# Moving the attention loop of a hybrid encoder layer into the hand-placed plan, with the S5 linear unit woven into its first two steps

## The chip, the cores and the metric

The kernel runs on one NeuronCore of one Trainium2 chip. The metric is the device time of one execution in microseconds (us); the time before is 1659.16 us, the median of three runs (1657.36 to 1663.84).

## What is computed

One post-norm layer over 1024 tokens of width 1024, all in fp32:

```python
h = layer_norm(x)
rq, rk, rv, rg, su, aq, ak, av = split(h @ w_in)
y_ret = retention(rq, rk, rv, rg, theta)              # 256 columns
y_ssm = s5_mixer(su, ...)                             # 256 columns
#   y = gelu(C states + D u);  y * sigmoid(y @ w_glu + b_glu)
y_att = window_sink_attention(aq, ak, av, sink)       # 512 columns
#   8 query heads on 2 key heads; a block of 128 queries sees its own and both
#   neighbouring key blocks; m = max(scores, sink);  p = exp(scores - m)
#   y = (p / (sum(p) + exp(sink - m))) @ v
h = layer_norm(alpha * h + concat(y_ret, y_ssm, y_att) @ w_out)
aff = softmax(h @ router_w)                           # 16 experts
# every expert takes its 128 tokens of highest affinity: SwiGLU, times gate, added back
h = layer_norm(alpha * h + experts(h))
```

## The kernel before

A matrix product that needs fp32 precision is made of three: each operand is split into a high and a low part (`split`, L60: ACT copies the high part, L65, and DVE subtracts it for the low part, L66), and `mm3` (L72) issues high·high, high·low and low·high (L74 to L76). TensorE also makes the transposes, into one PSUM tile `tp` of 128x512 (two buffers). PSUM has two buffers `at` for scores, two `mm` for projections, one `po` for attention values and one `sm` for the router.

The program has three parts. **The front**, `front()`, is a `Plan`: each operation is entered with `at(place, operation)`, and the sorted places are the program order of all engines, issued under a manual schedule. It ends with the units V0, o0, K0, o1, V1, o2, K1, o3: projections of keys and values, and four quarters of the S5 output (class `Output`). A quarter `o` multiplies transition tiles `MU` and `W` (L807, L810) with the saved states `Z`, which `Output.states` loads from DRAM (`s_d`) on SP's queue (L799). At places from `G` on come the S5 linear unit: `turn` (L822 transposes, L823 copies), `gate` (L828, two products), `gated` (tanh on ACT, L836; L837 and L838 on DVE give `YO`), `store` (L842, to `y_d`), and the splits of the output matrix `WO` (class `Matrix`, `parts`). The first scores of attention blocks 0 and 1 also stand there, and their exponentials behind the linear unit.

**The loop** in `build` (L2202 on) has no hand-made order: it lists 17 iterations, and the timeline scheduler orders each engine's instructions. A block i (0 to 15) is one chunk of 128 queries and one key head, four query heads. `attention_scores` makes the scores (L1310, L1311); DVE adds the slope bias and takes the maximum (L1314, called TTR below), then the negated maximum and the sink term (L1317, L1318). `attention_exp` is ACT's exponentials with their sums (L1328, L1330). `attention_out` has DVE add and invert the sums (L1340, L1341), ACT scale the probabilities (L1343), PE transpose them per key block (L1349) with a split into `pT`, PE multiply with the values (L1356), and ACT and DVE put the result in the rows `yh`, `yl` (L65, L66, L1362). `out_proj_load(t)` loads the retention and S5 columns of tile t and splits them into the same `yh`, `yl`; `out_proj_part(t, n)` makes one half of 512 columns, 8 chunks of three products, and DVE adds the residual into `z` (L1391) with its statistics (L1394); `router(t)` transposes `z` (L1444, L1446 into `rt`), multiplies with the router's weights (L1456), computes the affinities (L1464 to L1473), finishes the norm (L1478 gain, L1483 shift) and stores, with ACT's scaled copy `ah` (L1492) in the buffer of `rt`; `rank_tile(t)` counts for expert choice (L1584 to L1595). I write half (t, n) for an out-projection half; there are 14 in the loop, (0,0) to (6,1).

**The rest** is `last_tile` (tile 7) and the experts, again by hand: `for` each of 16 experts, load, split, multiply.

Of the kernel before, what the change touches and what calls it, by code (L numbers as in the profile page):

```python
# [764 lines left out]
class Output:  # L765


    def __init__(self, K, I):
# [61 lines left out]

    def gated(self, m, q):
# [107 lines left out]
def front(K, I, pool, close):  # L939
# [314 lines left out]
    at(G + 1.2, lambda: mat.parts(4))  # L1254
    at(G + 5.0, lambda: mat.parts(6))
# [40 lines left out]
def attention_scores(K, i):  # L1296

    nc = K.nc
    c, kv = divmod(i, 2)
    b0, b1 = max(c - 1, 0), min(c + 2, NT)  # L1300
    W, ro, k0 = (b1 - b0) * P, (b0 - c + 1) * P, b0 * P
    qs = K.Q.pop(i)
    sm = K.small.tile([P, 5, 4], F32, name="asm", bufs=3)
    m, nm, rs, es, rd = (sm[:, k] for k in range(5))
    hs = slice(kv * 4, kv * 4 + 4)
    S = []
    for g in range(4):
        h = kv * 4 + g
        ps = K.pat.tile([P, 512], F32, name="at")
        nc.tensor.matmul(ps[:, :W], qs[:, g, :], K.KHL[kv][:, 0, k0:k0 + W], start=True, stop=False)  # L1310
        nc.tensor.matmul(ps[:, :W], qs[:, g, :], K.KHL[kv][:, 1, k0:k0 + W], start=False, stop=True)  # L1311
        s = K.score[K.heads % 10]
        K.heads += 1
        nc.vector.tensor_tensor_reduce(s[:, :W], ps[:, :W], K.R[:, ro:ro + W], 2.0 ** -(h + 1),  # L1314
                                       K.sink[:, h:h + 1], OP.add, OP.max, accum_out=m[:, g:g + 1])
        S.append(s)
    nc.vector.tensor_scalar(nm, m, -1.0, None, op0=OP.mult)  # L1317
    nc.vector.tensor_tensor(es, K.sink[:, hs], m, OP.subtract)  # L1318
    K.P[i] = S, sm
# [12 lines left out]

def attention_out(K, i):
    nc = K.nc
    c, kv = divmod(i, 2)
# [8 lines left out]
    po = K.po.tile([P, 512], F32, name="po")
    pTs = []
    for b in range(b0, b1):
        pt = K.ptp.tile([P, 4, P], F32, name="tp")
# [4 lines left out]
        pTs.append(pT)
    for b in range(b0, b1):
        pT = pTs[b - b0]
        for s in range(2):
# [8 lines left out]

def out_proj_load(K, t):
    nc, pool = K.nc, K.op
    y = pool.tile([P, 4, P], F32, name="y")
    nc.sync.dma_start(y[:, 0:2, :], K.y_dram[t])
    for m in range(2):
        nc.sync.dma_start(y[:, 2 + m, :], K.y2_dram[m][:, t * P:(t + 1) * P])  # L1370
    z = pool.tile([P, D], F32, name="z", bufs=3)
    rows = nc.sync.dma_start(z, K.h_dram[t])
# [4 lines left out]
    return rows


def out_proj_part(K, t, n, c0=0, c1=KC):  # L1380

    nc = K.nc
    yh, yl, z = K.Y[t]
# [3 lines left out]
    for c in range(c0, c1):
        mm3(nc, K.ps, (yh[:, c], yl[:, c]), [K.WO[s][c // 4][:, c % 4, ns] for s in range(2)], c == 0, c == KC - 1)
    if c1 < KC:
        return  # L1390
# [945 lines left out]
```

## Time and profile before

| | |
|---|---|
| runs | 1659.16 us median; 1657.36, 1659.16, 1663.84 |
| profiled execution | 1658.7 us |
| its span (first to last instruction) | 1657.0 us |
| mean granted TensorE clock | 0.988 of 2.4 GHz |
| front, up to the last product of o3 | 0 to 280.7 us |
| from there to the first out-projection half | 280.7 to 324.2 us |
| halves (0,1) to (6,1) | 326.8 to 472.5 us |
| last tile and experts | 472.5 to 1657 us |

Read it with the clock in mind: the change touches 250 to 475 us of the 1657, and the busy shares of the whole span are those of the experts. "Busy" of TensorE (PE) is the union of its rows, each with the tail of a pipelined matmul.

### The profile page before, as it was taken

The numbers are of one execution on the slowest core, as the hardware profiler recorded it, in microseconds if no ns is written. First come the engines' busy times: TensorE is split into PE (matmuls) and PEld (weight loads), VectorE is DVE, ScalarE is ACT, GpSimd is POOL, SyncE is SP. The second block draws the span as 40 slices with busy tenths as digits, with TensorE's granted clock in tenths as the row PEclk, the third lists the DMA queues.
The fourth block names the chain that finished last, engine by engine and source line by source line (L and its number), as shares of the span: only waits on it lengthen the run. The fifth ranks groups of instructions, "written<-read, shape, count | busy, mean of one in ns | idle before, by whom it ended". The sixth has DMA issues, their size and how long they took to land.

```text
span 1657.0 us, 21108 instructions
## 1 busy us (share of the span) xinstructions
PE 1587.8 (96%) x7704; PEld 1288.8 (78%) x7704; DVE 1416.3 (85%) x1734; ACT 1129.3 (68%) x1272; POOL 211.4 (13%) x237
## 2 busy tenths in 40 slices
PE   7999998799988999999999999999999999999997
PEld 5888886687766788888888888888888778777785
DVE  7986954777889989888898888888888999999996
ACT  4644544775646678777777777777778777787773
POOL 3002110011010010110101001010011303231221
PEclk9999999899999999999999999999999999999998
DMA  5566485324228899999999999999999999999993
GB/s 190 186 168 143 114 234 179 128 78 159 69 103 314 341 376 407 394 365 381 365 391 385 356 386 367 396 372 360 396 370 404 399 392 409 388 414 380 389 418 141
DMA packets 102682, 505.74 MB, mean 305 GB/s; under 512 B 12977, under 2 KB 28081, under 8 KB 51890
## 3 DMA queue, kind: packets, MB, share of 16 engines
q1 hardware_dynamic: 87426, 476.60, 75.3%
q0 software_dynamic: 15152, 27.79, 6.2%
q8 instruction: 60, 0.98, 0.2%
q14 instruction: 44, 0.36, 0.1%
HBM read 461.36 MB, written 42.99 MB: 304 GB/s over the span
## 4 chain that ended last, share of the span: by engine, by line
PE 60%; DVE 15%; DMA 9%; issue 7%; ACT 7%; POOL 1%; SPq 0%; POOLq 0%; DVEq 0%; ACTq 0%
PE gu L1812 27%; PE y L1812 14%; DVE whl L1859 6%; DMA zz<-acc_d 4%; PE mm L74 4%; PE mm L76 4%; PE mm L75 4%; ACT whl L1852 3%; DMA wraw<-in_exp_w_down 2%; PE tp L1797 2%; DMA wraw<-in_exp_w_gate 1%; PE po L1356 1%; ACT S L1330 1%; DVE pT L66 1%; PE sm L1456 1%
## 5 line engine op out<-in xcount | busy, mean ns | idle before, releaser
L1859 DVE TENSOR_TENSOR whl<-wraw,whl 128x2048 fp32r<-128x2048 f32 x384 | 873.4, 2289 | 94.1 <-ACT whl L1852 93.8
L1852 ACT ACTIVATE whl<-wraw 128x2048 fp32r<-128x2048 f32 x384 | 734.8, 1917 | 240.1 <-PE gu L1812 86.6
L1812 PE MATMUL gu<-whl,xT 128*128 128x512 f32 x3072 | 740.1, 397 | 0.0
L1812 PEld LDWEIGHTS gu<-whl,xT 128*128 128x128 f32 x3072 | 570.8, 189 | 124.7
L1812 PE MATMUL y<-whl,hT 128*128 128x512 f32 x1536 | 368.6, 395 | 0.7 <-ACT hT L65 0.7
L1812 PEld LDWEIGHTS y<-whl,hT 128*128 128x128 f32 x1536 | 288.5, 188 | 69.6 <-ACT hT L65 0.9
L1786 POOL DMA_INDIRECT xs<-h_d,index x15 | 41.4, 2758 | 740.5 <-PE y L1812 552.2
L65 ACT ACTIVATE hT<-tp 128x512 fp32r<-128x512 f32 x80 | 46.1, 584 | 31.7 <-PE tp L1797 17.0
L74 PE MATMUL mm<-hT,whl 128*128 128x512 f32 x160 | 65.9, 412 | 0.0
L76 PE MATMUL mm<-hT,whl 128*128 128x512 f32 x160 | 62.9, 393 | 0.0
L75 PE MATMUL mm<-hT,whl 128*128 128x512 f32 x160 | 62.6, 391 | 0.0
L66 DVE TENSOR_TENSOR hT<-tp,hT 128x512 fp32r<-128x512 f32 x80 | 54.1, 684 | 7.3 <-ACT hT L65 7.3
L74 PE MATMUL mm<-WO,yh 128*128 128x512 f32 x128 | 52.1, 407 | 3.5 <-ACT yh L65 3.5
L1797 PE MATMUL tp<-ident,hid 128*128 128x128 f32 x256 | 39.7, 279 | 13.5 <-DVE hid L1894 13.4
L1797 PEld LDWEIGHTS tp<-ident,hid 128*128 128x128 f32 x256 | 31.6, 142 | 25.1 <-DVE hid L1894 17.8
L75 PE MATMUL mm<-WO,yh 128*128 128x512 f32 x128 | 50.9, 398 | 0.0
L76 PE MATMUL mm<-WO,yl 128*128 128x512 f32 x128 | 49.6, 398 | 0.0
L74 PE MATMUL mm<-whl,hT 128*128 128x512 f32 (+1 forms) x128 | 46.4, 362 | 0.0
L1330 ACT ACTIVATE S<-S,asm 128x384 f32<-128x384 f32 (+1 forms) x64 | 36.9, 578 | 13.1 <-DVE asm L1317 7.6
L1894 DVE TENSOR_TENSOR hid<-hid,gu 128x512 f32<-128x512 f32 x64 | 43.6, 681 | 1.9 <-PE gu L1812 1.9
L76 PE MATMUL mm<-whl,hT 128*128 128x512 f32 (+1 forms) x128 | 43.5, 340 | 1.2 <-DVE hT L66 1.2
L75 PE MATMUL mm<-whl,hT 128*128 128x512 f32 (+1 forms) x128 | 43.7, 341 | 0.8 <-DVE whl L130 0.8
(430 smaller groups left out, 1775.4 us busy)
## 6 DMA issues: line engine op xcount, KB each, us to landing
wraw<-in_exp_w_gate SPq DMA_DIRECT2D x128, 1024.0 KB, 8.0
wraw<-in_exp_w_up SPq DMA_DIRECT2D x128, 1024.0 KB, 7.8
wraw<-in_exp_w_down SPq DMA_DIRECT2D x128, 1024.0 KB, 8.0
wraw<-in_w_in SPq DMA_DIRECT2D x8, 1024.0 KB, 7.2
x<-in_x SPq DMA_DIRECT2D x8, 512.0 KB, 4.6
h_d<-x SPq DMA_DIRECT2D x8, 512.0 KB, 3.2
q_d<-kst SPq DMA_DIRECT2D x32, 128.0 KB, 2.7
wraw<-in_w_out SPq DMA_DIRECT2D x4, 1024.0 KB, 5.8
```

Source lines behind the costliest of these rows:

```text
L65: nc.scalar.activation(hi, src, AF.Copy)
L66: eng.tensor_tensor(lo, src, hi.bitcast(F32), OP.subtract)
L74: nc.tensor.matmul(ps, a[0], b[0], start=start, stop=False)
L75: nc.tensor.matmul(ps, a[0], b[1], start=False, stop=False)
L76: nc.tensor.matmul(ps, a[1], b[0], start=False, stop=stop)
L1330: nc.scalar.activation(S[g][:, :W], S[g][:, :W], AF.Exp, bias=nm[:, g:g + 1], accum_out=rs[:, g:g + 1])
L1786: nc.gpsimd.indirect_dma_start(out=xs, out_offset=None, in_=K.h1_dram, in_offset=bass.IndirectOffsetOnAxis(ap=K.index[:, e:e + 1], axis=0))
L1797: K.nc.tensor.transpose(pt[:, c, :], src[:, (c0 + c) * P:(c0 + c + 1) * P], K.ident)
L1812: nc.tensor.matmul(ps, a[s][c], u[:, t, i * w:(i + 1) * w], start=first and id(ps) not in began, stop=last and left[id(ps)] == 0)
L1852: self.K.nc.scalar.activation(u[:, 0, :], self.raw[k1].rearrange("p a b -> p (a b)"), AF.Copy)
L1859: self.K.nc.vector.tensor_tensor(u[:, 1, :], raw, u[:, 0, :].bitcast(F32), OP.subtract)
L1894: at(self.after, q, 3, lambda: nc.vector.tensor_tensor(self.h[q], self.h[q], self.pg[q][1], OP.mult))
```

## The change

The loop moves into the plan. Z is the place behind o3. A new class `Block` splits a block's work into `scores` (two heads at a time), `top`, `exp`, `norm`, `scale`, `turn`, `part`, `value` and `put`, each entered with a place of its own; step j (2 to 15) begins at place Z + 20 + 11(j - 2). In step j stand the scores of block j+2, norm and scale of block j+1, turn to put of block j, one out-projection half in three pieces (t = j//2 - 1, n = j mod 2), one half of the router work of the tile before it, and in even steps the rank of the tile before that. Blocks 0 and 1 and the linear unit share the places Z to Z + 20. The last tile's function takes over the rank of tile 5.

```diff
@@ Output, states and their loads
-    def states(self, g2, q, pool):
+    def states(self, g2, q, pool, **kw):
...
-        z = pool.tile([P, 2, 4, P], F32, name="Z")
+        z = pool.tile([P, 2, 4, P], F32, name="Z", **kw)
@@ front
     at(e2 + 7.0, lambda: out.states(*qs[0], X["s5m"][1]))
+    at(e2 + 7.1, lambda: out.states(*qs[1], K.ast, tag="k4", bufs=3))
...
-    at(O + 0.02, lambda: out.states(*qs[1], X["s5o"][1]))
...
-    for i, k in enumerate(mq):
-        at(G + 1.7 + i * 2.0, lambda k=k: out.gate(*k))
-        at(G + 3.7 + i * 2.0, lambda k=k: out.gated(*k))
-    at(G + 11.0, lambda: (out.store(0), out.store(1)))
-    at(G + 15.0, lambda: close(X["s5o"][0], X["s5m"][0]))
+    for k, a, b in zip(mq, (3.6, 5.3, 9.6, 13.7), (5.4, 7.1, 11.4, 15.5)):
+        at(Z + a, lambda k=k: out.gate(*k))
+        at(Z + b, lambda k=k: out.gated(*k))
+    at(Z + 15.6, lambda: (out.store(0), out.store(1)))
...
-    at(G + 1.2, lambda: mat.parts(4))
-    at(G + 5.0, lambda: mat.parts(6))
+    at(Z + 4.5, lambda: mat.parts(4))
+    at(Z + 10.0, lambda: mat.parts(6))
...
-        at(G - 0.2 + i * 1.1, lambda i=i: attention_scores(K, i))
-        at(G + 10.4 + i * 2.6, lambda i=i: attention_exp(K, i))
+    scored(0, Z - 0.2, Z - 0.1, Z + 1.6, Z + 2.5)
+    scored(1, Z + 2.6, Z + 2.7, Z + 4.0, Z + 7.3)
+    at(Z + 6.0, block[0].norm)
+    at(Z + 6.2, lambda: block[0].scale(nc.vector))
+    turned_over(0, (Z + 8.7, Z + 8.8), Z + 12.7, Z + 16.2)
+    scored(2, Z + 11.3, Z + 11.4, Z + 13.0, Z + 13.5)
...
+    at(Z + 16.0, loop_space)
...
+    for j in range(2, 2 * NT):
+        s = Z + 20.0 + 11.0 * (j - 2)
+        k, odd = divmod(j, 2)
+        if j + 2 < 2 * NT:
+            scored(j + 2, s, s + 4.2, s + 5.2, s + 5.6)
...
+            at(s + 0.05, block[j + 1].norm)
+            at(s + 2.4, block[j + 1].scale)
+        turned_over(j, (s + 0.7, s + 1.15, s + 4.1), s + 8.35, s + 9.7)
+        t = k - 1
+        cs = (4, 5, 6, 7, 0, 1, 2, 3) if j == 2 else range(KC)
+        for place, a, b in ((1.6, 0, 3), (5.3, 3, 6), (6.95, 6, 8)):
+            at(s + place, lambda t=t, odd=odd, cs=cs, a=a, b=b: out_proj_chunks(K, t, odd, cs[a:b], a == 0, b == KC))
+        at(s + 8.4, lambda t=t, odd=odd: out_proj_end(K, t, odd))
...
+        else:
+            at(s + 6.6, lambda t=k: out_proj_split(K, t))
...
+            at(s + 3.7, lambda t=t: router_turn(K, t, 0))
+            at(s + 6.9, lambda t=t: router_part(K, t, 0))
+            at(s + 9.75, lambda t=t: router_turn(K, t, 1))
...
+            at(s + 1.55, lambda t=t: router_part(K, t, 1))
+            at(s + 2.3, lambda t=t: logits(K, t))
+            at(s + 3.2, lambda t=t: out_proj_gain(K, t))
+            at(s + 4.3, lambda t=t: logits_exp(K, t))
+            at(s + 6.5, lambda t=t: logits_norm(K, t))
+            at(s + 6.6, lambda t=t: out_proj_shift(K, t))
+            at(s + 8.0, lambda t=t: out_proj_store(K, t))
...
+            at(s + 7.0, lambda t=t: (token_parts(K, t), rank_tile(K, t)))
@@ build
-    for i in range(2 * NT + 1):
-        if ahead <= i < 2 * NT:
...
-            attention_scores(K, i)
-            attention_exp(K, i)
```

`scored(i, a, b, c, d)` places a block's two pairs of scores, `top` and `exp`; `turned_over` its turns (each with its split 0.5 later), values and `put`. Other edits: the probabilities of blocks 0 and 1 are scaled by DVE (L1436 of the new file) in place of ACT; `g1`, `b1` and the first expert weights are loaded from places in steps 3 and 9; the split of `y` is apart from its load.

**SP's queue, the loads of Z.** Before, behind the last store of `roT`; the pair for o1 is the first two Z rows, and the pair for o0 stands some ten rows higher:

```order
L431 DMA y_d_72<-roT 128x256
L775 DMA wg<-in_ssm_w_glu 128x512
L777 DMA bg<-in_ssm_b_glu 128x2
L788 DMA MU<-m_d_94 128x512
L789 DMA MU<-u_d 128x512
L792 DMA W<-wo_d_86 128x576
L792 DMA W<-wo_d_88 128x576
L799 DMA Z<-s_d_89 128x512
L799 DMA Z<-s_d_91 128x512
L799 DMA Z<-s_d_90 128x512
L799 DMA Z<-s_d_92 128x512
```

Now the pair for o1 stands right behind that for o0:

```order
L890 DMA q_d_1_76<-kst 64x512 x4
L799 DMA Z<-s_d_89 128x512
L799 DMA Z<-s_d_91 128x512
L799 DMA Z<-s_d_89 128x512
L799 DMA Z<-s_d_91 128x512
L431 DMA y_d_70<-roT 128x256
L431 DMA y_d_71<-roT 128x256
L890 DMA q_d_1_78<-kst 64x512 x4
L903 DMA wraw<-in_w_out 128x2048
L431 DMA y_d_72<-roT 128x256
```

It has moved past the stores of `roT`, the store of keys (`kst`), a load of the output matrix and the loads of `wg` to `W`.

**ACT, the first two steps** (L836 is the linear unit's tanh, `WO` the split of the output matrix, L1330 and now L1425 the exponentials, L1343 the scale). Before:

```order
L65 ACTIVATE WO_3093<-wraw 128x1024 x2
L836 ACTIVATE glu<-mm,hb 128x512
L65 ACTIVATE WO_3093<-wraw 128x1024 x2
L836 ACTIVATE glu<-mm,hb 128x512 x3
L1328 ACT_TABLE_LOAD
L1328 ACTIVATE asm<-asm 128x4
L1330 ACTIVATE S,asm<-S,asm 128x256 x4
L1328 ACTIVATE asm<-asm 128x4
L1330 ACTIVATE S,asm<-S,asm 128x256 x4
L1343 ACTIVATE S<-S,asm 128x256 x8
```

Now, from the linear unit's second pair on:

```order
L836 ACTIVATE glu<-mm,hb 128x512 x2
L1423 ACTIVATE asm<-asm 128x4
L1425 ACTIVATE S,asm<-S,asm 128x256 x4
L65 ACTIVATE pT<-tp 128x512 x2
L65 ACTIVATE WO_3105<-wraw 128x1024 x2
L836 ACTIVATE glu<-mm,hb 128x512
L1423 ACTIVATE asm<-asm 128x4
L1425 ACTIVATE S,asm<-S,asm 128x384 x4
L836 ACTIVATE glu<-mm,hb 128x512
L65 ACTIVATE pT<-tp 128x512 x2
L65 ACTIVATE yh<-po 64x512
L1438 ACTIVATE S<-S,asm 128x384 x4
```

The exponentials of blocks 0 and 1, which stood behind the linear unit, now stand ahead of and between its rows; the last tanh stands behind the exponentials of block 2, and the first `put` (`yh<-po`) behind it.

**DVE, a step of the loop with `yl<-y`** (this row belongs to `out_proj_split`). Before, in the order of the scheduler:

```order
L1478 SCALAR_TENSOR_TENSOR z<-z,l1mv,g_3150 128x1024
L1404 TENSOR_SCALAR l1rs<-l1mv 128x1
L1314 ISA S,asm<-at,R,sink 128x384
L1314 ISA asm 128x1
L66 TENSOR_TENSOR yl<-y,yh 128x512
L1483 SCALAR_TENSOR_TENSOR z<-z,l1rs,b_3151 128x1024
L66 TENSOR_TENSOR yl<-po,yh 64x512
L1362 TENSOR_TENSOR yl<-po,yl 64x512
L1464 SCALAR_TENSOR_TENSOR nl<-rsum,l1mv,sm 128x16
L1465 SCALAR_TENSOR_TENSOR nl<-nl,l1rs,rsum 128x16
L1468 TENSOR_REDUCE rsm<-nl 128x1
L66 TENSOR_TENSOR pT<-tp,pT 128x512 x2
```

Now, in an even step (L1418 and L1419 are `top`, L1703 and L1706 the rank, L1500 and L1503 the half, L1464 ends `put`):

```order
L66 TENSOR_TENSOR pT<-tp,pT 128x512
L1418 TENSOR_SCALAR asm<-asm 128x4
L1419 TENSOR_TENSOR asm<-sink,asm 128x4
L66 TENSOR_TENSOR yl<-y,yh 128x512
L1703 TENSOR_SCALAR G,cnt<-rows,aff 128x128
L1706 SCALAR_TENSOR_TENSOR junk,cnt<-rows,aff,upto 128x128
L1500 SCALAR_TENSOR_TENSOR z<-z,mm 128x512
L1503 BN_STATS l1st<-z 128x6
L66 TENSOR_TENSOR yl<-po,yh 64x512
L1464 TENSOR_TENSOR yl<-po,yl 64x512
```

The row `yl<-y` now stands right behind `top` in every even step. On ACT its partner `yh<-y` stands there behind the five exponentials (L1423, L1425) that `top` releases; in odd steps `yh<-po`, the partner of the first row of `put`, stands behind the exponentials and `ah`.

## Rows read from the trace of the kernel before

**Rows 1.** The page, part 1: engine busy us (share of the span) xinstructions

```profile
PE 1587.8 (96%) x7704; PEld 1288.8 (78%) x7704; DVE 1416.3 (85%) x1734; ACT 1129.3 (68%) x1272; POOL 211.4 (13%) x237
```

**Rows 2.** Windows view: stretch, its us, busy us (x), PEclk, DMA share, GB/s

```profile
253.00:258.50 5.50, 0.00 (x1) 0.03 (x1) 3.76 (x7) 3.93 (x6) 0.00 (x0) 0.76 0.92 296
258.50:263.00 4.50, 4.50 (x23) 4.50 (x23) 1.40 (x2) 0.00 (x0) 0.00 (x0) 0.54 1.08 412
268.50:271.30 2.80, 2.80 (x26) 2.75 (x26) 0.00 (x0) 0.60 (x1) 0.00 (x0) 1.00 0.00 0
280.00:302.00 22.00, 12.94 (x58) 8.18 (x57) 17.59 (x43) 15.53 (x35) 2.91 (x9) 0.88 0.41 126
302.00:320.00 18.00, 17.38 (x81) 14.17 (x82) 12.84 (x36) 16.89 (x43) 1.53 (x2) 0.86 0.67 219
320.00:472.00 152.00, 143.80 (x770) 117.68 (x770) 117.33 (x312) 99.36 (x248) 15.59 (x39) 1.00 0.29 92
```

**Rows 3.** Timeline of PE at quarter o1: start, us, line, count, [idle before <-releaser]

```profile
258.50 1.27 PE L810 MATMUL mm<-W,Z 128*128 128x128 f32 x4 [5.72 <-DMA Z<-s_d]
```

**Rows 4.** Timeline of SP's DMA issues: the loads of Z

```profile
236.49 1.72 SPq L799 DMA_DIRECT2D Z<-s_d  x2
252.84 1.93 SPq L799 DMA_DIRECT2D Z<-s_d  x4
```

**Rows 5.** Timeline of PE: first scores, and first turn of probabilities

```profile
280.69 0.37 PE L1310 MATMUL at<-KHL,qs 128*128 128x256 f32 x1
301.91 1.33 PE L1349 MATMUL tp<-ident,S 128*128 128x128 f32 x5 [7.81 <-ACT S L1343]
```

**Rows 6.** Timeline of DVE: out-projection halves (0,1) and (6,1)

```profile
326.79 0.69 DVE L1391 SCALAR_TENSOR_TENSOR z<-z,mm 128x512 f32<-128x512 f32 x1 [0.89 <-PE mm L76]
...
472.45 0.67 DVE L1391 SCALAR_TENSOR_TENSOR z<-z,mm 128x512 f32<-128x512 f32 x1
```

**Rows 7.** Timeline of DVE: starts of neighbouring rows, and a wait for scores

```profile
305.21 0.61 DVE L1314 CUSTOM_DVE_ANT_0 S<-at,R,sink 128x384 f32<-128x384 f32 x1
305.75 1.28 DVE L66 TENSOR_TENSOR pT<-tp,pT 128x512 fp32r<-128x512 f32 x2
...
337.54 0.62 DVE L1314 CUSTOM_DVE_ANT_0 S<-at,R,sink 128x384 f32<-128x384 f32 x1 [2.08 <-PE at L1311]
```

**Rows 8.** Lines view, 320 to 472: line, shapes, count | busy, mean ns | idle <-releaser

```profile
L1330 ACT ACTIVATE S<-S,asm 128x384 f32<-128x384 f32 x40 | 24.2, 605 | 12.2 <-DVE asm L1317 6.7 <-DVE asm L1318 5.4
L1343 ACT ACTIVATE S<-S,asm 128x384 f32<-128x384 f32 x40 | 21.3, 605 | 1.9 <-DVE asm L1341 1.9
L65 ACT ACTIVATE yh<-y 128x512 fp32r<-128x512 f32 x6 | 3.8, 625 | 2.9 <-PE mm L75 2.1 <-ACT asm L1328 0.9
L1362 DVE TENSOR_TENSOR yl<-po,yl 64x512 fp32r<-64x512 f32 x14 | 9.7, 693 | 0.4
L1478 DVE SCALAR_TENSOR_TENSOR z<-z,l1mv,g 128x1024 f32<-128x1024 f32 x6 | 7.7, 1282 | 1.7 <-PE tp L1444 1.6
L1492 ACT ACTIVATE ah<-z 128x1024 f32<-128x1024 f32 x6 | 6.4, 1060 | 22.2 <-PE sm L1456 19.6 <-DVE yl L1362 2.5
L1464 DVE SCALAR_TENSOR_TENSOR nl<-rsum,l1mv,sm 128x16 f32<-128x16 f32 x6 | 1.4, 230 | 7.0 <-PE sm L1456 6.9
L1584 DVE TENSOR_SCALAR_CACHE_REDUCE G<-rows,aff 128x512 bf16<-128x512 f32 x1 | 0.7, 741 | 0.0
```

**Rows 9.** Lines view, 280 to 302: linear unit and WO splits

```profile
L66 DVE TENSOR_TENSOR WO<-wraw,WO 128x1024 fp32r<-128x1024 f32 x4 | 4.8, 1220 | 0.0
L838 DVE TENSOR_TENSOR YO<-glu,yT 128x512 f32<-128x512 f32 x4 | 4.4, 1098 | 0.1
L836 ACT ACTIVATE glu<-mm,hb 128x512 f32<-128x512 f32 x4 | 2.7, 684 | 4.7 <-DVE YO L838 2.8 <-PE mm L828 1.9
```

**Rows 10.** Timeline of SP: store of YO and the next issue

```profile
296.54 1.68 SPq L842 DMA_DIRECT2D y_d<-YO  x2
300.75 0.33 SPq L2206 DMA_DIRECT2D g<-in_ln_g  x1
```

More of the change, by code (lines that the diff above doesn't have):

```diff
@@ L1261, in front, with loop_space @@
     at(where["K1"] + 5.7, lambda: attention_space(K))
-    for i in range(2):
-        at(G - 0.2 + i * 1.1, lambda i=i: attention_scores(K, i))
-        at(G + 10.4 + i * 2.6, lambda i=i: attention_exp(K, i))
+    block = [Block(K, i) for i in range(2 * NT)]
+    def loop_space():
+        close(X["s5o"][0], X["s5m"][0])
+        X["op"], K.op = pool("op")
+        out_proj_load(K, 0)
+        K.g1 = K.op.tile([P, D], F32, name="g1")
+        K.b1 = K.op.tile([P, D], F32, name="b1")
+        K.X = Experts(K, I, O)
+        K.next_raw = lambda k: (K.raw if k < 4 or (k - 4) % 5 > 2 else K.raw2).tile([P, 2, 1024], F32, name="wraw")
+        X["tk"], K.tk = pool("tk")
+        rank_consts(K)
@@ new lines, in norm_rows, with scored, queries, turned_over @@
+    def norm_rows():
+        nc.sync.dma_start(K.g1, bcast(I["ln1_g"], D))
+        nc.sync.dma_start(K.b1, bcast(I["ln1_b"], D))
+    def scored(i, a, b, c, d):
+        v = block[i]
+        at(a, lambda: v.scores(0, 2))
+        at(b, lambda: v.scores(2, 4))
+        at(c, v.top)
+        at(d, v.exp)
+    def queries(place, i):
+        if i < 2 * NT:
+            at(place, lambda: attention_queries(K, i))
+    def turned_over(i, places, values, put):
+        v = block[i]
+        for b, place in zip(range(v.b0, v.b1), places):
+            at(place, lambda b=b: v.turn(b))
+            at(place + 0.5, lambda b=b: v.part(b))
+        for b in range(v.b0, v.b1):
+            at(values, lambda b=b: v.value(b))
+        at(put, v.put)
@@ L1293, in attention_consts @@
     nc.sync.dma_start(K.sink, bcast(I["attn_sink"], 8))
[L1296 to L1319, printed above, removed]
@@ L1365, in out_proj_load @@
 def out_proj_load(K, t):
     nc, pool = K.nc, K.op
[L1367 to L1372, printed above, removed]
+    K.y = pool.tile([P, 4, P], F32, name="y")
     yh = pool.tile([P, KC, P], F32R, name="yh", bufs=2)
     yl = pool.tile([P, KC, P], F32R, name="yl", bufs=2)
-    split(K, yh[:, 0:4, :], yl[:, 0:4, :], y)
@@ L1376, in out_proj_load, with out_proj_split, out_proj_chunks @@
-    K.Y[t] = yh, yl, z
[L1377 to L1383, printed above, removed]
+    z = pool.tile([P, D], F32, name="z", bufs=3)
+    nc.sync.dma_start(K.y[:, 0:2, :], K.y_dram[t])
+    for m in range(2):
+        nc.sync.dma_start(K.y[:, 2 + m, :], K.y2_dram[m][:, t * P:(t + 1) * P])
+    nc.sync.dma_start(z, K.h_dram[t])
+    K.Y[t] = yh, yl, z
+def out_proj_split(K, t):
+    yh, yl, _ = K.Y[t]
+    split(K, yh[:, 0:4, :], yl[:, 0:4, :], K.y)
+def out_proj_chunks(K, t, n, cs, first, last):
+    yh, yl, _ = K.Y[t]
@@ L1384, in out_proj_part, with out_proj_end @@
     ns = slice(n * 512, (n + 1) * 512)
-    if c0 == 0:
+    if first:
         K.ps = K.pmm.tile([P, 512], F32, name="mm")
[L1387 to L1390, printed above, removed]
+    for c in cs:
+        mm3(K.nc, K.ps, (yh[:, c], yl[:, c]), [K.WO[s][c // 4][:, c % 4, ns] for s in range(2)], first and c == cs[0],
+            last and c == cs[-1])
+def out_proj_end(K, t, n):
+    nc, z = K.nc, K.Y[t][2]
+    ns = slice(n * 512, (n + 1) * 512)
@@ L1456, in router_part, with logits @@
         K.nc.tensor.matmul(K.pr[t], K.rt[:, c, :], K.rw[:, 0, c, :], start=(c == 0), stop=(c == KC - 1))
-def affinities(K, t):
+def logits(K, t):
     nc, pool = K.nc, K.op
```

224 lines of the change are left out of this document (124 added, 100 removed).

## The prediction, written before the changed kernel had run

> **What bounds the kernel now.** I read the page first: PE is busy 96% of the span [rows 1], but most of that is the experts, which the change leaves alone. So the windows of the changed stretch come next [rows 2]. They show three regimes. Around quarter o1 PE does nothing for 5.5 us, then works 4.5 us at a granted clock of 0.54. From 280 to 302 us PE is busy 12.94 of 22 us, while DVE has 17.59 and ACT 15.53: the linear unit, the output matrix's splits and the first softmax hold PE up. From 320 to 472 us PE is busy 143.80 of 152 us at full clock, DVE 117.33 and ACT 99.36.
>
> Then I ask each regime for what ended its waits. At o1 it is a load: PE idles 5.72 us for Z [rows 3], and SP issued the first Z rows of that group at 252.84, the states of o0 already at 236.49 [rows 4]. Behind o3 (its last product ends where the first scores start, 280.69) PE has its longest wait, 7.81 us for ACT's scaled probabilities, at 301.91 [rows 5]. In the loop I use DVE's residual additions as milestones: half (0,1) at 326.79, half (6,1) at 472.45 [rows 6]. That is 145.66 us for 12 halves, 12.14 each. For comparison PE's busy time there is 143.80 / 152 x 12.14 = 11.5 us a half, an upper bound of its work, since a busy PE includes pipeline tails.
>
> The milestone of the whole sum is half (6,1): the last tile and the experts behind it keep their order, but for tile 5's rank, which moves there; that work stays DVE's and I cost it at nothing, since its DVE rows were already beside this tile's PE work. If DVE lacks room there it costs about 1 us.
>
> **Part 1, the load of Z for o1.** It moves from behind the output space to right behind o0's pair, into a buffer of the ring that the probabilities use later. At 236.49 + 1.7 it has about 20 us until 258.5. So the 5.72 us go [rows 3]. The clock should then not fall: o1's products ran 4.50 us at 0.54, the same number for o2 in 2.80 us at 1.00 [rows 2], 1.7 us more. DVE was busy 3.76 of the 5.5 idle us, with rows for which the next projection's PSUM tile has to wait in any case; I give back 0.6. Gain: 5.7 + 1.7 - 0.6 = 6.8 us; bounds 0 (something else holds it) and 7.4. So o3 ends at 273.9 in place of 280.69.
>
> **Part 2, the first two steps.** Times here count from o3's end. DVE's row order gives: eight TTRs of 256 columns, four splits of WO at 1.22, the linear unit's four products at 1.10 with an affine row of 0.42 before each [rows 9], the probabilities of two blocks scaled by DVE (eight rows of 256 columns, new on DVE; I take 0.25 each, a little over half the affine row of 512 columns; bounds 0.2 and 0.42), four splits of 0.6, and four TTRs of block 2, about 20 us, plus some 3 us until the first exponentials are there: `top` of block 2 at about 23. From there each piece waits for the one before on the other engine. Exponentials of block 2: four at 0.605 and a small one [rows 8], 2.5, to 25.7. The last tanh 0.68, affine row and product 1.5 [rows 9], to 27.9. Then `put` of block 0 writes into memory that the output loop takes over from the linear unit, so it waits for the store of YO: the trace shows 296.54 for the issue and 4.2 us until the next DMA into that memory could go [rows 10]; I take 3.3 (bounds 1.7, its issue, and 4.2), to 31.2. `put`, splits and block 2's norm 2.4; four TTRs 2.2; `top` and exponentials of block 3 2.7; `yh`, `yl` 2.0: 40.5, the start of step 2. Half (0,0) ends some 11 us into it and (0,1) at about 59. Before it ended at 326.79 - 280.69 = 46.1. **So the weave loses 13 us at this milestone**, though attention is then one block further ahead.
>
> Here a rule of the Trainium skill says otherwise: Perfetto Trace Analysis, section Optimization Strategy, advises interleaving regimes whose most contended engine differs. By it the linear unit would vanish beside the loop's PE work, and the milestone would come no later than 46. The trace doesn't bear out the condition: the linear unit's regime and the softmax of the first blocks lean on the same DVE and ACT [rows 2], and what fills PE, the out-projection, only begins behind the store. I keep 59.
>
> **Part 3, the steps.** Neighbouring DVE rows overlap a little (a TTR shows 0.61, the next row starts 0.54 later; two splits take 1.28 [rows 7]), so I take starts: 0.54 a TTR, 0.6 to 0.68 a 512-column row, 1.2 for the 1.28 of gain or shift [rows 8].
>
> Even step on DVE: two TTRs 1.08, norm 0.4, two splits 1.28. Then the second pair of scores stands on PE behind a turn that needs a `tp` buffer, which these splits free: 0.9 of waiting, an estimate (bounds 0, and 2.08, the longest wait of a TTR for scores that I saw [rows 7]). Two TTRs 1.08, split 0.68, `top` 0.2: 5.6. Now comes what the order makes new: `yl<-y` is next on DVE, its partner is ACT's copy behind five exponentials, 2.5 + 0.6 [rows 8]. **DVE stands 3.1 us**, to 8.7. `yl` 0.6, half 0.66, statistics 0.62, `put` 1.36: 12.0 us.
>
> Odd step: 2.76 as before, logits three rows of 0.23 [rows 8] 0.7, gain 1.2, TTRs 1.08, split and `top` 0.85, affinities 0.3, shift 1.2, half and statistics 1.5: 9.6. ACT started its exponentials at 6.5, is done at 9.0, makes `ah` (1.06 [rows 8]) and then `yh<-po`: 10.5. DVE stands 0.9, then 1.36: 11.9. The scale (four rows of 0.6 [rows 8]) lies on ACT in DVE's shadow. PE's 11.5 at most a half fits under both.
>
> Rank adds a row of up to 0.74 [rows 8] and its mask: 0.9 on average, in four even steps. Sum: steps 4 to 12 are 5 x 12.0 + 4 x 11.9 + 3.6 - 0.95 (block 14 has two key blocks) = 110.2. Step 3 has no router: 10.2. Step 13: 10.9. Step 14 has no scores and no exponentials (4.3 less TTR and wait, PE then decides): 8.8. Half (6,1) falls 3.8 into step 15, as PE is that far ahead. From the start of step 2: 12.0 + 10.2 + 110.2 + 10.9 + 8.8 + 3.8 = 155.9. So half (6,1) comes at 273.9 + 40.5 + 155.9 = 470.3, against 472.45: **2.2 us earlier**. Loads of `g1`, `b1` and expert weights move into steps 3 and 9; their cover is the loop's DMA share of 0.29 [rows 2].
>
> The profiled execution took 1658.7 us, so it would take 1656.5; the median stands 0.46 above, which gives **1657 us**, no change that a measurement (0.5%, 8.3 us) can tell.
>
> **Rivals.**
>
> 1. *Waits don't chain; PE sets the pace.* If DVE's stands shrink because the copies come sooner than I order them, steps go to PE's 11.5 or, without tails, near 10.5. Against my mean of 12.2 with rank over 11 steps that is 8 to 19 us: 1638 to 1649, say **1645, faster**. For it: PE's 143.80 of 152 [rows 2], and that DVE and ACT have slack. Against it: engines work in program order, and `yl<-y` stands where it stands. The skill's interleaving rule (above) would also end here: 13 us of the head back makes 1644.
>
> 2. *TensorE's clock falls in the loop, slower.* DVE's two stands leave PE without work in every step. Granted clock was 0.54 after the 5.72 us idle and 0.86 from 302 to 320, behind the wait of 7.81 [rows 2, 3, 5], against 1.00 in the loop where PE idles 8 of 152 us. It decides when 11.5 / clock exceeds 12.0: below a mean of 0.96. At 0.86 a step takes 13.4, 1.3 more, over 11 steps 14 us: **1671, slower**. Against it: the idle stays near 0.5 us a step, less than in 302 to 320. The Trainium skill (TensorE: Matmul & The Clock Gate, A second HAM failure mode) tells of a kernel whose short idles between groups of products made the clock go up and down; 320 to 472 us, with its idles and 1.00, doesn't show that here.
>
> 3. *The earlier load gains nothing*, because Z's ring buffer or another operand of o1 comes late: 6.8 us back, **1664**, no change that can be told. Its other operands `MU` and `W` are loaded ahead of both pairs; little speaks for it.
>
> **Numbers.** My forecast 0.53, rival 1 0.28, rival 2 0.10, rival 3 0.09. Errors of 0.4 us a step either way (11 steps, 4.4 us) and of Part 2's bounds (2 us) spread the forecast over 1650 to 1664. Faster by over 8.3 us needs 1650.8: nearly all of rival 1 and 0.04 of the forecast, 0.31. Slower, from 1667.5: rival 2 and 0.02 of the rest, 0.12. Range 1642 to 1667: it leaves out rival 2 and the lower part of rival 1, about 2 in 10; the forecast's own is 1650 to 1664.
>
> **What would show it.** Right: PE without idle in front of o1's products and clock 1.00 there; a DVE idle of about 3 us before `yl<-y` in each even step, ended by ACT's `yh`, and of about 1 us before the first row of `put` in odd ones; a wait for DMA before the first `yh<-po`; residual additions 12 us apart; (0,1) some 59 us behind o3, (6,1) near 470. Wrong: spacing near 11 with DVE's idles ended by PE (rival 1); PEclk under 0.95 between 340 and 460 (rival 2); an idle before o1 still ended by Z (rival 3).

## The result, and the profile after

The changed kernel took 1670.81 us (median of 10 runs), the kernel before, now also with 10 runs, 1662.35 us. The ratio over all these runs is 1.0057, interval 1.0036 to 1.0078: **about 9.5 us slower** (the medians alone differ by 8.5), where 1657 us and no change had been forecast, and outside the range of 1642 to 1667. Times below are compared by ratios, since the kernel before moved by 3 us with more runs. Milestones come from one profiled execution of each kernel.

Four of DVE's residual additions serve as milestones: halves (0,0), (6,0), (6,1) and (7,1), the last in the last tile. Kernel before, timeline of DVE ((6,1) and the end of o3 are in [rows 6] and [rows 5]):

```profile
324.22 0.69 DVE L1391 SCALAR_TENSOR_TENSOR z<-z,mm 128x512 f32<-128x512 f32 x1 [1.08 <-PE mm L76]
467.29 0.69 DVE L1391 SCALAR_TENSOR_TENSOR z<-z,mm 128x512 f32<-128x512 f32 x1 [0.21 <-PE mm L76]
492.59 0.69 DVE L1391 SCALAR_TENSOR_TENSOR z<-z,mm 128x512 f32<-128x512 f32 x1 [0.57 <-PE mm L76]
```

The changed kernel, timeline of PE (its first scores, where o3 ends):

```profile
274.11 0.72 PE L1409 MATMUL at<-KHL,qs 128*128 128x256 f32 x4
```

And the timeline of its DVE, the same additions:

```profile
326.43 0.68 DVE L1500 SCALAR_TENSOR_TENSOR z<-z,mm 128x512 f32<-128x512 f32 x1
472.63 0.68 DVE L1500 SCALAR_TENSOR_TENSOR z<-z,mm 128x512 f32<-128x512 f32 x1
480.50 0.69 DVE L1500 SCALAR_TENSOR_TENSOR z<-z,mm 128x512 f32<-128x512 f32 x1 [0.43 <-PE mm L76]
503.28 0.69 DVE L1500 SCALAR_TENSOR_TENSOR z<-z,mm 128x512 f32<-128x512 f32 x1 [1.31 <-PE mm L76]
```

So the time went here (us, differences of these rows):

| stretch | before | after | |
|---|---|---|---|
| up to the end of o3 | 280.69 | 274.11 | -6.6 |
| head: to half (0,0) | 43.53 | 52.32 | +8.8 |
| loop: (0,0) to (6,0) | 143.07 | 146.20 | +3.1 |
| end: (6,0) to (7,1) | 25.30 | 30.65 | +5.4 |
| half (7,1) at | 492.59 | 503.28 | +10.7 |

The work behind it has the same order. In the twelve profiles of this case it took 1164.4 us (before) to 1171.3 us, and the two profiles of one kernel, experiment 4, differ there by 2.9; 6.0 of the 16.7 by which the spans of the kernel before and the changed one differ lie there, and I read them as scatter.

The windows of the changed kernel answer to [rows 2]:

```profile
253.00:258.50 5.50, 4.70 (x33) 4.20 (x32) 3.48 (x7) 4.06 (x6) 0.00 (x0) 1.00 0.88 295
258.50:263.00 4.50, 4.50 (x26) 3.84 (x26) 1.69 (x2) 1.44 (x3) 0.00 (x0) 1.00 0.99 341
302.00:320.00 18.00, 8.39 (x32) 6.58 (x33) 11.37 (x29) 9.91 (x24) 1.58 (x7) 0.72 0.30 89
320.00:472.00 152.00, 140.55 (x753) 117.60 (x751) 110.99 (x300) 98.13 (x244) 15.92 (x40) 0.98 0.35 108
400.00:420.00 20.00, 17.86 (x89) 14.90 (x88) 16.58 (x46) 12.33 (x29) 2.40 (x5) 0.91 0.50 172
440.00:460.00 20.00, 18.03 (x98) 15.26 (x98) 14.50 (x47) 11.14 (x30) 0.00 (x0) 0.91 0.17 47
```

The idle at o1 and its half clock are gone. From 302 to 320 us PE, busy 17.38 of 18 us before, is busy 8.39: the head has a hole that was not there. In the loop PE, DVE and ACT all have less busy time in the same 152 us than before, and the granted clock, 1.00 throughout before, is 0.91 in two of the 20 us windows: in each lies a stretch at 1.2 GHz, half of the full clock.

The stands in the steps came as worked out. Changed kernel, DVE in steps 8 and 9: the wait for scores, for `yl<-y`, and for the first row of `put`:

```profile
392.26 0.62 DVE L1412 CUSTOM_DVE_ANT_0 S<-at,R,sink 128x384 f32<-128x384 f32 x1 [1.11 <-PE at L1409]
...
397.35 0.69 DVE L66 TENSOR_TENSOR yl<-y,yh 128x512 fp32r<-128x512 f32 x1 [3.19 <-ACT yh L65]
...
412.05 0.68 DVE L66 TENSOR_TENSOR yl<-po,yh 64x512 fp32r<-64x512 f32 x1 [0.94 <-ACT yh L65]
```

In the head, ACT's first `put` waits for the stores of YO (ACT's timeline, then that of SP's queue):

```profile
306.41 0.59 ACT L65 ACTIVATE yh<-po 64x512 fp32r<-64x512 f32 x1 [3.59 <-DMA y_d<-YO]
```

```profile
296.12 7.66 SPq L842 DMA_DIRECT2D y_d<-YO  x2
```

And PE's scores of block 3 wait for DVE, which stands behind it (PE's timeline):

```profile
309.44 1.65 PE L1409 MATMUL at<-KHL,qs 128*128 128x384 f32 x4 [9.41 <-DVE asm L1412]
```

PE stands 9.41 us, longer than the 7.81 of [rows 5], and for a chain that crosses the engines: the last tanh stands behind the exponentials of block 2, the second store waits for its YO, the first `put` for the store, and DVE's maxima of block 3 for the `put`.

### The profile page after: what moved, and what is told of

Its sections match the earlier page's. It is cut to its first block, busy times and chain, and to the rows that moved or that the text cites. A ratio compares the mean times of both kernels' runs of the same rounds, so it can differ in the third digit from the quotient of the medians.

```text
span 1673.7 us, 21077 instructions
## 1 busy us (share of the span) xinstructions
PE 1594.1 (95%) x7704; PEld 1294.7 (77%) x7704; DVE 1418.9 (85%) x1742; ACT 1127.4 (67%) x1264; POOL 210.0 (13%) x237
## 4 chain that ended last, share of the span: by engine, by line
PE 59%; DVE 16%; DMA 12%; issue 6%; ACT 6%; POOL 1%; SPq 0%; POOLq 0%; DVEq 0%; ACTq 0%
PE gu L1931 26%; PE y L1931 13%; DVE whl L1978 6%; DMA wraw<-in_exp_w_down 5%; PE mm L74 4%; PE mm L76 4%; PE mm L75 4%; DMA zz<-acc_d 3%; ACT whl L1971 2%; DMA wraw<-in_exp_w_gate 2%; PE tp L1916 2%; DVE S L1412 1%; ACT S L1425 1%; PE tp L1445 1%; DMA wraw<-in_exp_w_up 1%
## 5 line engine op out<-in xcount | busy, mean ns | idle before, releaser
L74 PE MATMUL mm<-WO,yh 128*128 128x512 f32 x128 | 54.7, 427 | 0.6 <-ACT yh L65 0.6
L76 PE MATMUL mm<-WO,yl 128*128 128x512 f32 x128 | 52.3, 409 | 0.7 <-DVE yl L1464 0.7
L75 PE MATMUL mm<-WO,yh 128*128 128x512 f32 x128 | 52.1, 407 | 0.0
L2013 DVE TENSOR_TENSOR hid<-hid,gu 128x512 f32<-128x512 f32 x64 | 43.5, 680 | 1.8 <-PE gu L1931 1.8
L1438 ACT ACTIVATE S<-S,asm 128x384 f32<-128x384 f32 (+1 forms) x56 | 29.1, 589 | 22.9 <-DVE asm L1430 22.9
```

Source lines behind the costliest of these rows:

```text
L74: nc.tensor.matmul(ps, a[0], b[0], start=start, stop=False)
L75: nc.tensor.matmul(ps, a[0], b[1], start=False, stop=False)
L76: nc.tensor.matmul(ps, a[1], b[0], start=False, stop=stop)
L1438: self.K.nc.scalar.activation(self.S[g], self.S[g], AF.Copy, scale=rd)
L2013: at(self.after, q, 3, lambda: nc.vector.tensor_tensor(self.h[q], self.h[q], self.pg[q][1], OP.mult))
```

## The experiments

Milestones of all runs, from the same rows (head, loop and end as above):

| kernel | head | loop | end | ratio to before, interval |
|---|---|---|---|---|
| before | 43.5 | 143.1 | 25.3 | |
| changed | 52.3 | 146.2 | 30.7 | 1.0057, 1.0036 to 1.0078 |
| 1 split late | 50.3 | 147.8 | 30.7 | one run |
| 2 all stands late | 50.3 | 137.9 | 34.2 | 1.0022, 1.0002 to 1.0041 |
| 3 scores ahead of the router's turn | 52.0 | 142.8 | 29.3 | one run |
| 4 early load alone | 45.1 | 141.9 | 25.3 | 0.9964, 0.9948 to 0.9981 |
| 5 early gates | 49.8 | 146.2 | 30.0 | one run |
| 6 late put | 49.2 | 144.8 | 29.3 | one run |
| 7 rank first | 52.1 | 146.2 | 28.7 | one run |
| 8 all moves | 47.4 | 138.6 | 28.9 | 0.9966, 0.9944 to 0.9987 |
| 9 all moves, norm halved | 47.5 | 136.3 | 30.2 | 0.9972, 0.9950 to 0.9993 |
| 4 again | 45.1 | 141.0 | 25.3 | 0.9939, 0.9919 to 0.9959 |

Some rows differ without an edit in that stretch. Experiment 6 changes nothing from step 2 on, and its loop is 1.4 us shorter than the changed kernel's; experiments 3 and 6 leave the end as it is, and it is 1.4 us shorter. In each of these places the changed kernel has a stretch at half clock that the other lacks (rows below). A single profile has to be read with that in mind.

**1. The split of y late.**

```diff
-            at(s + 6.6, lambda t=k: out_proj_split(K, t))
+            at(s + 8.9, lambda t=k: out_proj_split(K, t))
```

> The changed kernel with one place moved: the split of y (ACT yh<-y, DVE yl<-y) goes from 6.6 to 8.9 in even steps, behind the residual addition. Theory (the order's own waits: DVE stands 3.19 us because its next row has its partner behind five exponentials): steps 2 and 4 lose most of the stand and get 1.5 to 2.5 us shorter, until the half's products end them. From step 6 on the rank row is DVE's next row and waits for the row of affinities, which ACT copies behind the same exponentials, so those steps keep a stand of about 3 us and their length within 0.3 us. Halves (0,1) to (6,1): about 4 us less than 144.3. Rival (TensorE sets the pace of the steps): no step gets shorter by more than 0.5 us and (0,1) to (6,1) stays at 144.

From the start of one step's maxima to the next, step 2 fell from 12.29 to 11.16 and step 4 from 12.16 to 11.92; step 6 stayed at 12.8. DVE no longer stands for `yh`, but in step 4 for TensorE's half, and from step 6 on for the row of affinities (the second row is step 6's):

```profile
346.72 0.69 DVE L1500 SCALAR_TENSOR_TENSOR z<-z,mm 128x512 f32<-128x512 f32 x1 [2.83 <-PE mm L76]
...
371.06 0.35 DVE L1703 TENSOR_SCALAR_CACHE_REDUCE G<-rows,aff 128x128 bf16<-128x128 f32 x1 [3.21 <-ACT rows L1720]
```

The second half of the theory holds (the next row inherits the stand), the first not: of 3.19 us only 1.1 and 0.24 were worth anything. Another wait of nearly the same length lay under it. Halves (0,1) to (6,1) took 145.37 us, 1.0 more than the 144.34 of the changed kernel where about 4 less was forecast: step 2's gain lies ahead of (0,1), and steps 8 to 12 were 14.45, 13.85 and 14.12 in place of 12.84, 14.79 and 13.61, with stretches at half clock in steps 8 and 12 here, in 10 and 12 there.

**2. Everything that DVE stands for late.**

```diff
-            at(s + 6.6, lambda t=k: out_proj_split(K, t))
+            at(s + 8.9, lambda t=k: out_proj_split(K, t))
-            at(s + 8.0, lambda t=t: out_proj_store(K, t))
+            at(s + 9.8, lambda t=t: out_proj_store(K, t))
-            at(s + 7.0, lambda t=t: (token_parts(K, t), rank_tile(K, t)))
+            at(s + 9.72, lambda t=t: (token_parts(K, t), rank_tile(K, t)))
```

> The changed kernel with every row that DVE stands for moved behind the work that is ready: split of y to 8.9, rank to 9.72, the store with ACT's ah to 9.8 (load of the next tile behind it). Theory (the order's own waits): no stand of 3 us before the residual addition, none of 0.9 us before put; even steps 1.8 us shorter, odd ones 0.9: (0,1) to (6,1) about 144.3 - 6 x 1.8 - 5 x 0.9 = 129 us, time 12 to 15 us below the changed kernel, so 3 to 6 us below the kernel before. Rival (TensorE sets the pace, 11.5 us of busy time a half): (0,1) to (6,1) not below 138, time at most 6 us below the changed kernel.

(0,1) to (6,1) took 136.88, between 129 and 138. The odd steps did as expected, 11.1 from 12.0. The even ones did not: with rank they are still 12.4 to 13.5, and DVE stands in each for TensorE:

```profile
394.98 0.69 DVE L1500 SCALAR_TENSOR_TENSOR z<-z,mm 128x512 f32<-128x512 f32 x1 [2.84 <-PE mm L76]
```

So the theory holds for odd steps and the rival for even ones. Of the 7.5 us that (0,1) to (6,1) lost, some 2.4 are the two falls of the clock, which are absent here. The end grew by 3.5 us: step 14's rank and step 15's store now run into the last tile, where PE waits 4.22 us and the clock has 0.88 from 480 to 500. With these moves only up to step 13 and the rank first, in experiment 8, the end is 28.9. The time, 1.0022, is about 6 us below the changed kernel, where the rival had at most 6 and the theory 12 to 15.

**3. Scores ahead of the router's turn.**

```diff
-            scored(j + 2, s, s + 4.2, s + 5.2, s + 5.6)
+            scored(j + 2, s, s + (4.2 if odd else 3.75), s + 5.2, s + 5.6)
-        turned_over(j, (s + 0.7, s + 1.15, s + 4.1), s + 8.35, s + 9.7)
+        turned_over(j, (s + 0.7, s + 1.15, s + (4.1 if odd else 3.65)), s + 8.35, s + 9.7)
-            at(s + 3.7, lambda t=t: router_turn(K, t, 0))
+            at(s + 4.3, lambda t=t: router_turn(K, t, 0))
```

> The changed kernel with TensorE's order in even steps changed: turn of the third key block first (3.65), then the second pair of scores (3.75), then the router's turn (4.3). Theory (one wait for a transpose buffer ahead of the scores in place of two): DVE's wait for scores falls from 1.1 to about 0.2 us, PE's idle of 1.2 to 2.1 us in each even step to about 1, even steps get 0.7 us shorter, (0,1) to (6,1) about 4 us less than 144.3; if the dips of the granted clock (0.91 in 400 to 420 and 440 to 460) come from these idles, they go, for 1.5 to 3 us more. Rival: the time returns as a wait of the last split for ACT behind the scale, no step changes by more than 0.2.

The loop fell by 3.4 us. DVE's wait for scores went from 1.11 to 0.51 (0.2 was forecast), and steps 6 and 8 from 12.76 and 12.84 to 12.18 and 12.25. One of the two falls of the clock stayed (0.91 from 400 to 420), the one in step 12 is gone. But it is gone in experiment 6 too, where the order of the loop is the changed kernel's (second row):

```profile
440.00:460.00 20.00, 18.53 (x110) 15.98 (x111) 16.17 (x48) 13.43 (x38) 0.00 (x0) 1.00 0.16 46
...
440.00:460.00 20.00, 20.00 (x116) 16.89 (x114) 15.56 (x44) 13.95 (x39) 1.19 (x4) 1.00 0.14 57
```

Step 12 took 13.61 us in the changed kernel, 12.28 in experiment 6 and 11.93 here. So 1.3 of the 1.7 us go with the clock, and that this edit removes the fall isn't shown; the order itself is worth 0.4 there, and 0.6 in steps 6 and 8.

**4. The early load alone**, in the kernel before.

```diff
     at(e2 + 7.0, lambda: out.states(*qs[0], X["s5m"][1]))
+    at(e2 + 7.1, lambda: out.states(*qs[1], K.ast, tag="k4", bufs=3))
-    at(O + 0.02, lambda: out.states(*qs[1], X["s5o"][1]))
```

> The kernel before with the early load of Z for o1 alone. Theory: PE's idle of 5.72 us at o1 and the half clock behind it go, o3 ends at about 274.1 instead of 280.69, and all of it is carried: half (7,1) at about 486, time 6 to 7 us below the kernel before. Rival (the first steps hang on ACT and DVE work, which does not move with PE): at most 2 us are left at half (0,1).

o3 ends at 274.02 and (7,1) comes at 486.34, 6.25 earlier than before; the time is 0.9964. Nearly all of the term is carried: 6.25 of 6.67 us. A second measurement, beside experiment 9, gave 0.9939, with (7,1) at 485.91; the milestones of both put the load's worth at 6 to 7 us, and the rest of the second ratio's 10 us is not accounted for:

> The kernel before with the early load of Z alone once more, beside the version with halves on the same chip: 0.996 of the kernel before, half (7,1) at 486; the theory has it 3 us above the version with halves, the rival level with it or below.

**5 and 6. Two edits of the head.** The fifth has the last gates earlier, the sixth `put` of block 0 later:

```diff
-    for k, a, b in zip(mq, (3.6, 5.3, 9.6, 13.7), (5.4, 7.1, 11.4, 15.5)):
+    for k, a, b in zip(mq, (3.6, 5.3, 7.5, 9.35), (5.4, 7.1, 9.4, 11.2)):
-    at(Z + 15.6, lambda: (out.store(0), out.store(1)))
+    at(Z + 11.25, lambda: (out.store(0), out.store(1)))
```

> The changed kernel with the last two gates of the linear unit at 7.5 and 9.35 (from 9.6 and 13.7), their tanh rows at 9.4 and 11.2 and the stores behind them. Theory (the first put waits for the store of YO): the last YO row comes at about 297 instead of 302.35, the store lands 5 us earlier, the first yh<-po goes at about 302 instead of 306.41, half (0,0) 4 us earlier, at about 322.5. Rival (ACT's and DVE's rows fill the head, whatever their order): half (0,0) within 1 us of 326.4.

```diff
-    turned_over(0, (Z + 8.7, Z + 8.8), Z + 12.7, Z + 16.2)
+    turned_over(0, (Z + 8.7, Z + 8.8), Z + 12.7, Z + 18.8)
```

> The changed kernel with put of block 0 at 18.8 instead of 16.2, so that norm, scale and the scores' maxima of blocks 2 and 3 stand ahead of the wait for the store of YO. Theory (that wait stands in front of work that is ready): the maxima of block 3 start at about 304.6 instead of 308.76, PE's idle of 9.41 becomes about 5, half (0,0) is 3 to 4 us earlier, at about 323. Rival (the out-projection needs that put anyway, the wait only moves): half (0,0) within 1 us of 326.4.

Counted from the end of o3, the head got 2.6 and 3.1 us shorter, not the 4 and 3 to 4 expected: the theory, a little less. (In the fifth o3 ended 1.4 us later than in the changed kernel, so half (0,0) itself came at 325.31, only 1.1 earlier.) In the fifth the last YO row starts at 295.92 and the first `put` no longer waits for a DMA, but DVE then stands elsewhere, 3.15 us for ACT's split behind the exponentials of block 2. In the sixth the maxima of block 3 start at 304.71, as expected, and PE's idle is 5.36.

**7. The rank of tile 5 first in the last tile.**

```diff
+    token_parts(K, t - 1)
+    rank_tile(K, t - 1)
     for q in range(2):
         router_turn(K, t, q)
...
-    token_parts(K, t - 1)
-    rank_tile(K, t - 1)
```

> The changed kernel with the rank of tile 5 ahead of the router's turns in the last tile. Theory (its turn of the affinities waits behind two turns whose copies wait for the store of ah): PE's idle of 2.48 us and DVE's 0.66 there go, halves (6,1) to (7,1) take 20.3 instead of 22.8 us. Rival (the rank's own 4 us of DVE rows are the cost, in whatever place): 22.3 or more.

(6,1) to (7,1) took 20.82 in place of 22.78, 0.5 more than expected. The changed kernel's row that it removes:

```profile
484.75 0.47 PE L1695 MATMUL tp<-ident,aff 128*128 128x128 f32 x1 [2.48 <-ACT rt L1561]
```

The number agrees with the theory, but not all of it is the place. The changed kernel's clock falls to half behind this wait (0.91 from 480 to 500); experiments 3 and 6, whose end has the changed kernel's order and the same wait (2.49 and 2.48), have no such fall, and they took 21.39 us. Windows of the changed kernel and of experiment 6:

```profile
480.00:500.00 20.00, 16.66 (x92) 13.49 (x92) 15.66 (x42) 8.81 (x13) 3.64 (x11) 0.91 0.26 105
...
480.00:500.00 20.00, 17.95 (x103) 14.13 (x103) 16.28 (x41) 7.18 (x12) 5.03 (x8) 1.00 0.23 82
```

So of the 2.64 us that this stretch lost against the 20.14 before, 1.4 go with the clock, 0.6 are the rank's place, and 0.7 are left, its own work or something else.

**8. All moves together** (split, rank and store late up to step 13).

> The changed kernel with all moves together: late split, rank and store in steps up to 13, TensorE's order of the third experiment, early gates, late first put, rank first in the last tile. Theory (the plan's stands add up): half (0,0) near 321, (0,1) to (6,1) near 134, (6,1) to (7,1) near 20.5, so (7,1) at about 486 and the time 16 us below the changed kernel, equal to the kernel before with the early load alone (0.9964 of the kernel before). Rival (TensorE's own work paces the steps once the stands are gone): (0,1) to (6,1) not below 138 and time at most 10 us below the changed kernel.

1658.38 us, 0.9966 of the kernel before, and (7,1) at 488.79. (0,1) to (6,1) is 136.0, between theory and rival again. Against the changed kernel this is about 15 us, at (7,1) and by the ratios: the order of the plan cost that much, some 3 to 4 us of it through the falls of the clock, as far as these two profiles tell. It is level with the early load alone.

**9. And the norm in halves.**

```diff
+            at(s + 5.3, lambda t=t: (out_proj_gain(K, t, slice(0, 512)), out_proj_shift(K, t, slice(0, 512))))
...
-            at(s + 3.2, lambda t=t: out_proj_gain(K, t))
+            at(s + 3.2, lambda t=t: out_proj_gain(K, t, slice(512, D)))
-            at(s + 6.6, lambda t=t: out_proj_shift(K, t))
+            at(s + 6.6, lambda t=t: out_proj_shift(K, t, slice(512, D)))
```

> All moves together as before, and gain and shift of the norm cut in two halves of 512 columns: the first halves go to 5.3 in the even step, where DVE stands 3.2 us for TensorE's half, the second halves stay in the odd step. Theory (after the stands are gone, odd steps hang on DVE's own rows and even steps on TensorE): odd steps 11.1 to about 10.0, even ones unchanged, DVE's wait before the even residual addition 3.2 to about 1.9, (0,1) to (6,1) 136 to 130, half (7,1) at about 483, time about 5 us below the version with all moves and 3 us below the early load alone. Rival (TensorE's work fills a pair of steps, 23.4 us, in any case): the odd steps' gain is given back in the even ones, (0,1) to (6,1) 134 or more.

Steps 7, 9 and 11 fell only from 11.1 to 10.5 (step 5 stayed), and (0,1) to (6,1) took 133.74: just below the rival's bound of 134. DVE, with 1.2 us moved out of the odd step, now stands for TensorE in odd steps too (1.75 us in step 8; the row is step 9's half):

```profile
402.58 0.69 DVE L1501 SCALAR_TENSOR_TENSOR z<-z,mm 128x512 f32<-128x512 f32 x1 [0.36 <-PE mm L76]
```

PE is busy 147.52 of the 152 us there, against 140.55 in the changed kernel:

```profile
320.00:472.00 152.00, 147.52 (x810) 124.17 (x809) 125.22 (x336) 103.30 (x253) 20.51 (x46) 1.00 0.37 114
```

At 11.1 us a half DVE waits for TensorE at every residual addition from (0,0) to (5,1): TensorE's work is the pace there. Half (7,1) came at 489.96, not at the 483 forecast; 2.0 of the difference is o3's later end in this profile, and 1.3 a fall of the clock in the end, 0.91 from 480 to 500. The time, 0.9972, is not better than the early load alone, measured beside it at 0.9939: no version here is faster than the scheduler's loop with one load moved, and only experiment 8 is level with it. The plan's loop in this form is 5 us shorter, its head 2.4 and its end 5 us longer.

## Why the prediction was wrong

**Right.** Part 1: forecast 6.8, seen 6.6, and carried nearly whole (experiment 4). Part 3's chain: the stands were forecast as 0.9, 3.1 and 0.9 us and were 1.11, 3.19 and 0.94. The steps were forecast as 12.0 and 11.9 us plus rank; steps 2 to 9 and 11 came within 0.3 us of their terms. The weave does lose time in the head; forecast was half (0,1) at 59, it came at 62.05.

**Wrong.** Half (6,1) was forecast at 470.3 and came at 480.50. The stands, the mechanism that I forecast, are there; what failed are four terms of the sum, three in these 10.2 us and one behind the milestone. About half of two of them is a clock that I had left at 1.00:

- *The head, "40.5, the start of step 2"*: 42.8, 2.3 us more, 2.5 with o3's end. `top` of block 2 came at 24.3 where I had 23 (the first maxima began only 1.1 us behind o3's end), so the last YO row ended at 29.3, not 27.9. From there to the first `put` it took 3.0 us, near my 3.3, so that went at 32.3 where I had 31.2. Then the maxima of block 3 took 3.0 us in place of 2.2, with DVE waiting for scores, and its `top` and exponentials 3.0 in place of 2.7; the granted clock of that window was 0.72.
- *The steps, "5 x 12.0 + 4 x 11.9 + 3.6 - 0.95"*: steps 2 to 12 took 137.0 instead of 132.4. Of the 4.6 us, 3.55 lie in steps 10 (14.79 instead of 12.9) and 12 (13.61 instead of 11.95), and both have a stretch of half clock. With the same order of the loop and no fall there, step 10 takes 13.76 (experiments 5 and 7) and step 12 takes 12.28 (experiment 6): 2.4 us are the clock. That was rival 2, which I had priced at 14 us for the whole loop and given 0.10; its sign, PEclk under 0.95 between 340 and 460, came in two windows, while the mean from 320 to 472 is 0.98. But the falls stand behind waits of PE of about 2 us for a transpose buffer (2.14 us at 415.56, ended by DVE's split), and not in DVE's two stands, as the rival had it. In step 12 it shows as a wait of DVE for the row of affinities, 1.25 us, which experiment 6 does not have. The rest of step 10 is the widest rank of the loop, 1.6 us of rows where I took a mean of 0.9.
- *"Step 14 ... 8.8, half (6,1) falls 3.8 into step 15"*: steps 13 to (6,1) took 26.6 instead of 23.5. Step 14 has the rank of tile 4, which none of my terms has, and DVE waits 2.63 us for its row of affinities, where no maxima are left to cover it: 10.5 us in place of 8.8. In step 15 the half comes 5.1 us behind the start, not 3.8: DVE's own rows ahead of it take 4.7, and TensorE's products end 0.4 later still.
- *"That work stays DVE's and I cost it at nothing"*: (6,1) to (7,1) took 22.78 instead of 20.14. At full clock the same order takes 21.39, so 1.4 of the 2.6 go with the clock and 1.25 are left for the rank and its place; moving it first got 0.6 of them back (experiment 7). The cover I named, TensorE's work, was itself waiting behind two turns.

-2.2 forecast, + 10.2 and + 2.6 are the 10.7 at half (7,1). Some 3.8 us of these 12.8 are the three falls of the clock in this one profile.

Two readings of mine were loose without changing the result. I called the products of o1 behind the idle the same number as those of o2; they are 22 and 24, so the half clock cost a little more than 1.7 us. And the affine row of 0.42 us is not among [rows 9], though the trace has it (0.413 to 0.424).

**The rivals.** Rival 1, that TensorE sets the pace, did not come, but it bounded the repairs of the loop: in experiment 1 the 3.19 us stand hid a 2.83 us wait for TensorE. Rival 2 came in part, as said. Rival 3 fell with the changed kernel's o3 and with experiment 4. The Trainium skill (Perfetto Trace Analysis, Optimization Strategy) says that interleaving regimes may improve performance. I had read that as (0,1) no later than 46; at 62.05, and still 57.8 with the head repaired, this weave did not bear it out. The loop had 1.00 before the change, and the changed one shows two falls of its clock behind waits of about 2 us. The Trainium skill's page TensorE: Matmul & The Clock Gate (A second HAM failure mode) tells of such short idles and a clock that goes up and down; the trace agrees, but only for some of these waits, as shown below.

**Open.** What is left of the end, 3.4 to 4.9 us in experiments 7 to 9, and 2.3 of the head were not taken apart further. A plan whose linear unit stays ahead of the loop, without the weave, was not run, so the head's loss is not split between the weave and its order. Whether a given idle brings a fall of the clock was not settled, nor how many of the ten runs have one.

## What to carry to other kernels

When an order is fixed by hand, walk each engine's rows once and ask of each what stands in front of its partner on the other engine; a row whose partner is queued behind a long group stands still, whatever its place in the table says. Before moving it, ask what the next wait is: a 3.19 us stand here was worth 1.1 us in one step and 0.24 in another, because a wait for TensorE of nearly the same length lay under it. Before you credit an edit with a gain seen in one profile, look at the same stretch in a profile of a kernel that has the same order there: here 1.3 us in step 12 and 1.4 us in the last tile came and went without an edit. And measure the parts of a large change one by one: here the load moved alone gave 0.9964, and the load with the repaired new loop 0.9966.

## What the runs showed of the hardware

The granted clock's falls to half in the loop didn't follow the idle in front of them simply. In the changed kernel PE stood 2.02 us at 390.61, and the window 380 to 400 has 1.00; it stood 2.14 us at 415.56, and 400 to 420 has 0.91. In experiment 1 it was 2.03 us at 389.02 with 0.91 and 2.15 us at 415.56 with 1.00. Experiments 2, 8 and 9, whose idles between 320 and 440 stay at or below 1.17 us, have 1.00 in all windows from 320 to 440.

The changed kernel and experiments 5, 6 and 7 have the same order from step 3 to step 13. In step 8 PE stands 2.02 us in all four: no fall in the changed kernel and in 6, a fall in 5 and 7. In step 12 it stands 1.97 us in all four: a fall in the changed kernel, 5 and 7, none in 6. Even one kernel differs from execution to execution: in experiment 4 PE stands 0.98 us at 399.68, and 399 to 403 has 0.57; in its second profile it stands 0.98 us at 400.20, and the same stretch has 1.00. A fall made step 8 1.0 us longer (13.83 and 13.85 against 12.84 and 12.83) and step 12 1.3 us (13.61 to 13.63 against 12.28).
